# Two heads at a time in the attention of a two-block float32 transformer kernel

## The chip, the cores and the metric

One core of one Trainium2 chip. The metric is device microseconds of one execution of the whole kernel. The engines are named as in the profile: PE (TensorE matmul), PEld (TensorE weight load), DVE (VectorE), ACT (ScalarE), POOL (GpSimd), SP (SyncE, which issues the loads).

## What is computed

Two transformer blocks of two layers each, on 256 tokens of 1024 features. The second block has two streams (latent and context). Only the attentions matter here; each has 8 heads.

```python
# first block, kind 0: sliding window with sinks; kind 1: causal over one block of 256 tokens (both with ALiBi)
logits = einsum('bnqhgd,bnkhd->bnhgqk', q, k) * 64 ** -0.5      # 64 features a head
p = exp(logits - m); out = einsum('bnhgqk,bnkhd->bnqhgd', p / denom, v)
# second block, per stream: 96 features in q and k, 64 in v; the latent stream sees the context's keys too
s = einsum('bqhd,bkhd->bhqk', q, k) * 96 ** -0.5
o = einsum('bhqk,bkhd->bqhd', softmax(s), v)
```

In the second block attention runs three times: context (256 keys) and latent (512 keys) in layer 0, latent (512 keys) in layer 1. In layer 1 the context gives keys and values alone.

## The kernel before

All weights stream from memory in chunks of eight 128 x 128 tiles. `Weights.get` loads chunks ahead (SP), ACT rounds each to `wh` (L302) and DVE forms the rest `wl` (L261), three chunks ahead of use. A product of the stream (`mm3`) is three float32r matmuls of a weight tile with 256 or 512 tokens, so a chunk is 24 matmuls; all matmuls go through one helper and stand at L373.

Work that does not use weights runs on the side. `tick()` is called at each new chunk and moves every generator in `self.sides` one `yield` further; what a generator issues is put behind the last matmul of the stream (`issue_after`), and the framework's scheduler then sets the order of the instructions on each engine. `attn1` (L924) and `attn2` (L1285) are such generators. `finish` drives one to its end.

Before, `attn1` takes one head per tick. In tick s it issues the logits of head s (tile `lg`: a matmul with 128 and one with 256 columns, with 64 rows of the array, rows 0 to 63 or 64 to 127 by the head's partition `p0`), its softmax on DVE and ACT (`softmax_step`), the three 128 x 128 transposes of head s-2 (`pt`, L940) with ACT's copy to `pts`, and the values of head s-3 (`pv`: a matmul with 256 and one with 128 columns, whose 64 output columns of the array are 0 to 63 or 64 to 127 by `op`). Two heads share a bank of `pv`, which is split into `yah`, `yal` or `ych`, `ycl` after the second.

`attn2` takes one head and one block of 128 queries per tick, 16 in all: one or two logit matmuls of 256 columns on 96 rows, softmax, two or four transposes (L1313), two or four value matmuls of 128 columns into 64 output columns. These matmuls are float32: the profile shows each of them as two MATMUL records, and each transpose as one.

PSUM banks: `at` (logits) has 2 buffers, `st` (transposes) and `pv` one each, `mm` (the stream) four.

The lines of one tick of `attn1` that the text speaks of:

```python
self.mm(lg[:, :P], qa[:, :P], ka[:, :P], True, True)
self.mm(lg[:, P:], qa[:, P:], ka, True, True)
...
self.mm(o, v[0][:, vc:vc + 64], t[:, :T], True, False)
self.mm(o[:, P:], v[1][:, vc:vc + 64], t[:, 2 * P:], False, True)
```

Of the kernel before, what the change touches and what calls it, by code (L numbers as in the profile page):

```python
# [19 lines left out]
P = 128  # L20
D = 1024
# [13 lines left out]
# hidden tiles of the second block's first feed-forward that the context makes ahead, and its groups  # L35
# [4 lines left out]
# column tiles of the first block's w_in  # L40
# [3 lines left out]
# column tiles of the second block's w_in (kr padded to a tile)  # L44
# [4 lines left out]
# the order of the second block's branches (0: convolution, 1: attention, 2: Fourier)  # L49
# [3 lines left out]
# ---------------------------------------------------------------- layout on the host  # L53
# [5 lines left out]
def _chunks(blocks):  # L59
    """[n, 128, 128] tiles in order of use -> [n / 8, 128, 1024]"""  # L60
    a = np.concatenate(blocks, axis=0)
    n = a.shape[0]
    return a.reshape(n // 8, 8, P, P).transpose(0, 2, 1, 3).reshape(n // 8, P, 8 * P)


def _km(t, ms, ks=None):
    """k outer"""
    ks = range(t.shape[0]) if ks is None else ks
    return np.stack([t[k, m] for k in ks for m in ms])


def _mk(t, ms, ks=None):
    """k inner"""
    ks = range(t.shape[0]) if ks is None else ks
    return np.stack([t[k, m] for m in ms for k in ks])
# [26 lines left out]
def _head_cols(w, perm):  # L102
    """the columns of w in blocks of 64, permuted"""
    k, m = w.shape
    return w.reshape(k, m // 64, 64)[:, perm].reshape(k, m)
# [7 lines left out]
def _pack_weights(i):  # L113
    """all weights but w_ada, as tiles of 128 x 128 in the order in which the core uses them"""
# [48 lines left out]
def _cols(v):  # L163
    """a vector over features -> [128, n / 128]"""
    return v.reshape(-1, P).T
# [7 lines left out]
def _pack_vectors(i):  # L173
    """small vectors by partition; their columns by name"""
# [18 lines left out]
def _tables():  # L193
    """constants that depend on shapes alone"""
# [30 lines left out]
# ---------------------------------------------------------------- the program  # L225
class Weights:
    """The stream of weight chunks: loads and splits run ahead of the products."""
# [38 lines left out]
    def catch_up(self):  # L266
        """the split that was held back, if any"""
# [12 lines left out]
class Kernel:  # L280
# [12 lines left out]
    # -- instructions  # L293
# [42 lines left out]
    # -- order of work  # L336
    def after_root(self):
        """work that can wait stays out of the steps of a root"""
        return self.tc.issue_after(self.last_root.ins) if self.last_root else contextlib.nullcontext()
# [40 lines left out]
    # -- operands in two parts  # L380
    def split_pair(self, name, src, scale=1.0):
        """hi, lo [128, 2, 256] of scale * src"""
# [12 lines left out]
    def split_affine(self, hi, lo, src, bias):  # L395
        """of src + bias, bias by partition"""
# [3 lines left out]
    # -- products  # L400
    def linear(self, nm, xs, ks, done, first_outer=0, name="mm"):
        """nm column tiles of weights against xs (a list of (hi, lo) [128, 256] by k); two column
        tiles to a bank; done(i, bank, n) for each bank. The first first_outer tiles k outer."""
# [21 lines left out]
    def linear_tiles(self, xs, ks, done, name="mm", outer=False, hold=False):  # L425
        """as linear, for D features; done(m, psum) takes each column tile, the last two of which
        have a bank each; with outer, the first four go k outer; with hold, the
        split ahead of the last chunk is left to the norm that follows"""
# [21 lines left out]
    # -- statistics over features  # L450
    def rsqrt(self, nv, n=2, keep=False):
        """(-nv) ** -0.5 from the exponent's half by a step of third order, z' = z (u^2 + 10/3 s^2 u + 5 s^4)
        with u = nv z^2, and one of second order, z' = z (u + 3 s^2); each step's z is s times the root,
        with s' = 8/3 s^5 and s' = 2 s^3, 1 in the end"""
# [21 lines left out]
    def colsum(self, parts, tag="st"):  # L476
        """sums over partitions (features) of one or two tiles [128, 256]: [128 tokens, 2]"""
# [9 lines left out]
    def spread(self, out, v):  # L487
        """[128 tokens, 2] -> the same row of 256 tokens on all partitions"""
# [3 lines left out]
    # ------------------------------------------------------------ setup  # L492
    def setup(self):
# [3 lines left out]
        # x first  # L497
# [36 lines left out]
    def ada_plan(self, l, lo, hi, every, wait=None):  # L534
        """jobs that make columns lo to hi of layer l's modulation vectors: outputs on partitions,
        summed over k; one each `every` ticks"""
# [35 lines left out]
    def ada_ready(self, l, i):  # L572
        """what the i-th (shift, scale) of layer l is used as"""
# [12 lines left out]
    def ada_gate(self, l, i):  # L586
        """the i-th gate of layer l"""
# [23 lines left out]
    # ------------------------------------------------------------ feed-forward products  # L611
    def ffn_act(self, name, bank, tmp, j):
        """silu(gate) * up of one hidden tile (gate and up in one bank) into half j of tmp"""
# [4 lines left out]
    def ffn_single(self, name, xs, outer, add, before_last=lambda: None):  # L618
        """one stream of 256 tokens; add(m, psum) takes each part of the result"""
# [34 lines left out]
    def ffn_both(self, name, us, add, ctx_done=lambda: None):  # L654
        """both streams (512 tokens); us by k: (hi, lo) [128, 2, 256]"""
# [12 lines left out]
        def gu_outer(hs):  # L668
            """the context's stream first, then the latent one on the same weights"""
# [72 lines left out]
    def ffn_early(self, n, tiles):  # L742
        """the context's hidden tiles that fill the latent stream's n-th norm"""
# [14 lines left out]
    def ffn_rest(self, name, us, uc, add, ctx_done):  # L758
        """both streams, with the context's first hidden tiles made ahead"""
# [61 lines left out]
    # ------------------------------------------------------------ first block  # L821
# [3 lines left out]
    def layer_norm_add(self, m, psum, scale_x):  # L825
        """tile m of scale_x + psum; its deviation from the mean of the first six tiles"""
# [38 lines left out]
    def layer_norm_end(self, gname, bname, l, xs, last):  # L865
        """the norm; operands in two parts (or the last layer's result in f32), and the residual"""
# [29 lines left out]
    def softmax_step(self, kind, h, logits, cols, l):  # L896
        """rows of one head for both query blocks: [128 q, 128 + 256 keys]"""
# [26 lines left out]
    def attn1(self, kind, l, heads, q, k, v, out):  # L924
        """heads: (head, q pair, q half, partition, k, v columns, output tile, its partition)"""
        ps, pts, pv = {}, {}, {}
        n = len(heads)
        for s in range(n + 3):
            if s < n:
                h, qt, p0, kt = heads[s][:4]  # L930
                lg = self.bank("at", "lg").rearrange("p a b -> p (a b)")[:, :384]
                qa, ka = q[qt][p0:p0 + 64, :], k[kt][p0:p0 + 64, :]
                self.mm(lg[:, :P], qa[:, :P], ka[:, :P], True, True)
                self.mm(lg[:, P:], qa[:, P:], ka, True, True)
                ps[s] = self.softmax_step(kind, h, lg, 384, l)
            if 0 <= s - 2 < n:
                z = ps.pop(s - 2)
                pt = self.bank("st", "pt").rearrange("p a b -> p (a b)")[:, :384]
                for c, (a, b) in enumerate(((0, 0), (P, 0), (2 * P, 0))):
                    self.nc.tensor.transpose(pt[:, c * P:(c + 1) * P], z[:, a:a + P], self.ident)  # L940
                t = self.slot("pts").rearrange("p a b -> p (a b)")[:, :384]
                self.act(t, pt, AF.Copy)
                pts[s - 2] = t
            if 0 <= s - 3 < n:
                i = s - 3
                vc, ot, op = heads[i][4:]
                t = pts.pop(i)
                if i % 2 == 0:
                    pv[0] = self.bank("pv", "pv")[:, 0, :]
                o = pv[0][op:op + 64, :]  # L950
                self.mm(o, v[0][:, vc:vc + 64], t[:, :T], True, False)
                self.mm(o[:, P:], v[1][:, vc:vc + 64], t[:, 2 * P:], False, True)
                if i % 2 == 1:
                    self.split_into(out[0][ot // 2][:, ot % 2, :], out[1][ot // 2][:, ot % 2, :], pv[0])
            yield

    def mixer1(self, l, xs, xa):
        """the first block's mixer and its norm; xs: operands by k, xa: residual"""
# [61 lines left out]
        # gated short convolution  # L1020
# [47 lines left out]
        # branches, merged  # L1068
# [84 lines left out]
    # ------------------------------------------------------------ second block  # L1153
# [3 lines left out]
    def rms_add(self, s, h, last=False):  # L1157
        """one tile [128, 256] more of the sum of squares"""
# [25 lines left out]
    def ada_apply(self, s, i, h, b, hi, lo, ks=range(KD)):  # L1184
        """operands of norm(h) * g * (1 + scale) + shift"""
# [8 lines left out]
    def rms_all(self, s):  # L1194
        """the squares of an input that is all there"""
# [22 lines left out]
    def low_norm(self, name, src, nk, g, nfeat, key):  # L1218
        """operands of a norm over the latent features of src (f32 tiles [128, 256])"""
# [24 lines left out]
    def kv_values(self, xs):  # L1244
        """values by token: [128 tokens, 512] for each of two blocks"""
# [16 lines left out]
    def key_rope(self, src, kt, lat):  # L1262
        """the shared rotary key (rows 64-95 of src, its permuted copy in 96-127) to all heads"""
# [7 lines left out]
    def rope_rows(self, out, src):  # L1271
        """rows 64-95 of out [128, n, 256]: src * cos + permuted src * sin"""
# [12 lines left out]
    def attn2(self, q, keys, vals, out, first):  # L1285
        """q, keys: by pair of heads [96, 2, 256]; vals: blocks of 128 tokens [128, 512]"""
        nk = len(keys)
        scale = 96.0 ** -0.5
        n = 16
        ps, pts, pv = {}, {}, {}  # L1290
        for s in range(n + 3):
            while s < n and len(q) < max(s // 4 + 1, first):
                yield
            if s < n:
                h, qb = divmod(s, 2)
                lg = self.bank("at", "lg2")
                qa = q[h // 2][0:96, h % 2, qb * P:(qb + 1) * P]
                for c in range(nk):
                    self.mm(lg[:, c, :], qa, keys[c][h // 2][0:96, h % 2, :], True, True)
# [476 lines left out]
```

## Time and profile before

| what | value |
|---|---|
| three runs, median (lowest to highest) | 2974.29 us (2972.76 to 2975.88) |
| profiled execution, span | 2972.9 us, 1.4 us under the median of the runs |
| PE, PEld, DVE, ACT, POOL busy | 99%, 92%, 69%, 45%, 4% |
| granted clock of TensorE, mean | 0.997 |
| attention in the first block, layer 0 and 1 | 33.1 to 126.4 us, 509.3 to 602.3 us (start of its first and last burst of matmuls) |
| attention in the second block | 1355.2 to 1434.2, 1574.9 to 1673.9, 2584.6 to 2683.2 us |

No time of the profiled execution itself is given beside its span; the median stands 1.4 us above it, which is taken as what lies around the span. The busy time of PE is a sum of modelled durations that overlap, so what an instruction costs PE is read from the distance between the starts of the instructions around it.

### The profile page before, as it was taken

What the parts mean: (1) busy time and instruction counts of PE and PEld (TensorE: products, weight loads), DVE (VectorE), ACT (ScalarE), POOL (GpSimd) and SP (SyncE); (2) the same over time, 40 slices, a digit from 0 to 9 for tenths busy, and PEclk for the clock granted to TensorE, in tenths of its full rate; (3) what the DMA queues carried; (4) which work ended last, traced back from release to release, by engine and by line L of the source; (5) the groups of instructions that cost most, each with busy time, mean ns of one, the idle gap of its engine ahead of it and who ended that gap; (6) DMA issues with size and microseconds to landing.
All of it is one profiled execution on the core that took longest, in us unless ns stands there. A gap on an engine that the chain in (4) does not pass through costs nothing. (4 is left out here: it accounts for less than half of the span.)

```text
span 2972.9 us, 51535 instructions
## 1 busy us (share of the span) xinstructions
PE 2935.0 (99%) x21000; PEld 2731.8 (92%) x21000; DVE 2065.2 (69%) x3506; ACT 1340.9 (45%) x2100; POOL 108.1 (4%) x121
## 2 busy tenths in 40 slices
PE   8999999999999999999999999999999999999999
PEld 7899999799999999999998998888888888989998
DVE  6779667647756787788888685555675557867655
ACT  6545444644544422246556552222322224665444
POOL 1001001000001000010010000000100001000000
PEclk9999999999999999999999999999999999999999
DMA  7565655354655665544453353443354543425453
GB/s 260 174 230 171 224 197 169 114 170 157 203 181 170 226 226 169 167 157 142 157 177 107 129 181 132 134 135 120 104 188 162 169 156 114 163 93 164 163 184 107
DMA packets 134589, 486.66 MB, mean 164 GB/s; under 512 B 14928, under 2 KB 15184, under 8 KB 134352
## 3 DMA queue, kind: packets, MB, share of 16 engines
q1 hardware_dynamic: 133776, 482.58, 49.0%
q8 instruction: 165, 2.70, 0.4%
q10 hardware_dynamic: 576, 0.79, 0.1%
q14 instruction: 72, 0.59, 0.1%
HBM read 482.26 MB, written 1.05 MB: 163 GB/s over the span
## 5 line engine op out<-in xcount | busy, mean ns | idle before, releaser
L302 ACT ACTIVATE wh<-raw 128x1024 fp32r<-128x1024 f32 x765 | 809.5, 1059 | 1260.4 <-issue 272.2
L261 DVE TENSOR_TENSOR wl<-raw,wh 128x1024 fp32r<-128x1024 f32 x765 | 939.3, 1230 | 500.6 <-ACT wh L302 492.4
L547 DVE SCALAR_TENSOR_TENSOR junk<-ada,cb 128x1024 bf16<-128x1024 f32 x256 | 313.6, 1225 | 3.6 <-DMA ada<-in_w_ada_dram 1.4
L373 PE MATMUL f<-xh,wh 128*128 128x256 f32 x704 | 199.0, 283 | 0.0
L373 PE MATMUL f<-xl,wh 128*128 128x256 f32 x704 | 198.9, 283 | 0.0
L373 PE MATMUL f<-xh,wl 128*128 128x256 f32 x704 | 197.4, 280 | 0.0
L373 PE MATMUL g<-xh,wh 128*128 128x256 f32 x608 | 173.9, 287 | 8.5 <-ACT wh L302 7.0
L373 PE MATMUL g<-xh,wl 128*128 128x256 f32 x608 | 173.8, 286 | 0.7 <-DVE wl L261 0.7
L373 PE MATMUL g<-xl,wh 128*128 128x256 f32 x608 | 173.1, 285 | 0.6 <-DVE xl L308 0.6
L373 PE MATMUL bg<-wh,wh 128*128 128x256 f32 x576 | 168.5, 292 | 0.0
L373 PE MATMUL bg<-wh,wl 128*128 128x256 f32 x576 | 162.7, 282 | 0.0
L373 PE MATMUL bg<-wl,wh 128*128 128x256 f32 x576 | 162.1, 281 | 0.0
L373 PE MATMUL b<-uh,wh 128*128 128x512 f32 (+1 forms) x384 | 145.7, 380 | 0.0
L373 PE MATMUL a<-uh,wh 128*128 128x512 f32 (+1 forms) x384 | 145.4, 379 | 0.0
L373 PE MATMUL a<-wh,wl 128*128 128x256 f32 x512 | 144.9, 283 | 0.0
L373 PE MATMUL a<-wh,wh 128*128 128x256 f32 x512 | 144.7, 283 | 0.0
L373 PE MATMUL a<-uh,wl 128*128 128x512 f32 (+1 forms) x384 | 144.1, 375 | 0.0
L373 PE MATMUL b<-uh,wl 128*128 128x512 f32 (+1 forms) x384 | 144.0, 376 | 0.0
L373 PE MATMUL a<-ul,wh 128*128 128x512 f32 (+1 forms) x384 | 143.7, 374 | 0.0
L373 PE MATMUL a<-wl,wh 128*128 128x256 f32 x512 | 143.5, 280 | 0.0
L373 PE MATMUL b<-ul,wh 128*128 128x512 f32 (+1 forms) x384 | 143.4, 374 | 0.0
L1169 POOL TENSOR_TENSOR sq<-sq,sq 128x256 f32<-128x256 f32 x63 | 64.5, 1030 | 2143.2 <-ACT sq L302 2141.9
(429 smaller groups left out, 8774.2 us busy)
## 6 DMA issues: line engine op xcount, KB each, us to landing
raw<-in_w_dram SPq DMA_DIRECT2D x765, 512.0 KB, 3.3
ada<-in_w_ada_dram SPq DMA_DIRECT2D x144, 512.0 KB, 3.9
hc<-in_ctx_dram SPq DMA_DIRECT2D x8, 256.0 KB, 6.0
x<-in_x_dram SPq DMA_DIRECT2D x4, 256.0 KB, 6.9
out_dram<-out SPq DMA_DIRECT2D x4, 256.0 KB, 2.4
cb<-in_c_dram SPq DMA_DIRECT2D x1, 512.0 KB, 8.3
cb<-in_c_ctx_dram SPq DMA_DIRECT2D x1, 512.0 KB, 8.4
dft<-in_dft_dram ACTq DMA_DIRECT2D x2, 256.0 KB, 4.2
```

The lines of the kernel that those rows point to most:

```text
L261: self.last_split = kb.nc.vector.tensor_tensor(lo.rearrange("p a b -> p (a b)"), raw, f.bitcast(F32), ALU.subtract)
L302: return self.nc.scalar.activation(out, in_, func, **kw)
L373: return self.nc.tensor.matmul(out, a, b, start=start, stop=stop)
L547: self.nc.vector.scalar_tensor_tensor(junk, raw, 1.0, self.cb[:, s, :], ALU.mult, ALU.mult, accum_out=self.mods[:, l, s, c:c + 1])
L1169: self.nc.gpsimd.tensor_tensor(r["q"], r["q"], q[:, 0, :], ALU.add)
```

## The change

`attn1` takes a pair of heads every two ticks. In the first tick of a pair it issues four logit matmuls that alternate between the two heads (one on rows 0 to 63, one on rows 64 to 127, each head into a bank of its own), both softmaxes, the transposes of the first head of the pair before, and the four value matmuls of the pair before that, which alternate between the two heads (output columns 0 to 63 and 64 to 127). The second tick has the transposes of the second head alone. `while self.ticks % 2 != kind` lets the two attentions of a layer begin their pairs on different ticks. `attn2` does the same with the two heads of `hp` on one block of queries: its logits are not alternated (96 rows), its values are, chunk by chunk. The same instructions are issued in all; elsewhere only line numbers, comments and docstrings differ. The core of the diff:

```diff
     def attn1(self, kind, l, heads, q, k, v, out):
-        ps, pts, pv = {}, {}, {}
-        n = len(heads)
-        for s in range(n + 3):
+        ps, pts = {}, {}
+        n = len(heads) // 2
+
+        def turn(i):
+            z = ps.pop(i)
+            pt = self.bank("st", "pt").rearrange("p a b -> p (a b)")[:, :384]
+            for c in range(3):
+                self.nc.tensor.transpose(pt[:, c * P:(c + 1) * P], z[:, c * P:(c + 1) * P], self.ident)
+            t = self.slot("pts").rearrange("p a b -> p (a b)")[:, :384]
+            self.act(t, pt, AF.Copy)
+            pts[i] = t
+
+        while self.ticks % 2 != kind:
+            yield
+        for s in range(n + 2):
             if s < n:
-                h, qt, p0, kt = heads[s][:4]
-                lg = self.bank("at", "lg").rearrange("p a b -> p (a b)")[:, :384]
-                qa, ka = q[qt][p0:p0 + 64, :], k[kt][p0:p0 + 64, :]
-                self.mm(lg[:, :P], qa[:, :P], ka[:, :P], True, True)
-                self.mm(lg[:, P:], qa[:, P:], ka, True, True)
-                ps[s] = self.softmax_step(kind, h, lg, 384, l)
+                pair = heads[2 * s:2 * s + 2]
+                lgs = [self.bank("at", "lg").rearrange("p a b -> p (a b)")[:, :384] for _ in pair]
+                for qa, ka in (((0, P), (0, P)), ((P, T), (0, T))):
+                    for (h, qt, p0, kt, *_), lg in zip(pair, lgs):
+                        o = lg[:, :P] if qa[0] == 0 else lg[:, P:]
+                        self.mm(o, q[qt][p0:p0 + 64, qa[0]:qa[1]], k[kt][p0:p0 + 64, ka[0]:ka[1]], True, True)
+                for j in range(2):
+                    ps[2 * s + j] = self.softmax_step(kind, pair[j][0], lgs[j], 384, l)
+            if 0 <= s - 1 < n:
+                turn(2 * s - 2)
             if 0 <= s - 2 < n:
...
-                self.mm(o, v[0][:, vc:vc + 64], t[:, :T], True, False)
-                self.mm(o[:, P:], v[1][:, vc:vc + 64], t[:, 2 * P:], False, True)
-                if i % 2 == 1:
-                    self.split_into(out[0][ot // 2][:, ot % 2, :], out[1][ot // 2][:, ot % 2, :], pv[0])
+                pair = heads[2 * s - 4:2 * s - 2]
+                ts = [pts.pop(2 * s - 4 + j) for j in range(2)]
+                o = self.bank("pv", "pv")[:, 0, :]
+                for (*_, vc, ot, op), t in zip(pair, ts):
+                    self.mm(o[op:op + 64, :], v[0][:, vc:vc + 64], t[:, :T], True, False)
+                for (*_, vc, ot, op), t in zip(pair, ts):
+                    self.mm(o[op:op + 64, P:], v[1][:, vc:vc + 64], t[:, 2 * P:], False, True)
+                self.split_into(out[0][ot // 2][:, ot % 2, :], out[1][ot // 2][:, ot % 2, :], o)
             yield
+            if 0 <= s - 1 < n:
+                turn(2 * s - 1)
+            yield
...
     def attn2(self, q, keys, vals, out, first):
...
+                lgs = [self.bank("at", "lg2") for _ in range(2)]
+                for j in range(2):
+                    qa = q[hp][0:96, j, qb * P:(qb + 1) * P]
+                    for c in range(nk):
+                        self.mm(lgs[j][:, c, :], qa, keys[c][hp][0:96, j, :], True, True)
...
+            if 0 <= s - 1 < n:
+                turn(2 * s - 2)
             if 0 <= s - 2 < n:
...
                 for c in range(2 * nk):
...
+                    for j in range(2):
+                        self.mm(pv[64 * j:64 * j + 64, qb * P:(qb + 1) * P],
+                                vals[c][:, 64 * (2 * hp + j):64 * (2 * hp + j) + 64],
+                                ts[j][:, c * P:(c + 1) * P], c == 0, c == 2 * nk - 1)
...
             yield
+            if 0 <= s - 1 < n:
+                turn(2 * s - 1)
+            yield
```

What this moves on PE, at three places. The rows are PE's program (line, output<-inputs, size of the output); a float32 matmul is one row here and two records in the profile.

First block, layer 0, sliding window, the tick in which logits and values stand together. Before: one head's logits, then one head's values, then the stream (`g`).

```order
L373 MATMUL lg_568<-qk_381,qk_383 128x128
L373 MATMUL lg_568<-qk_381,qk_383 128x256
L373 MATMUL pv_595<-pts_530,va_390 64x256
L373 MATMUL pv_595<-pts_530,va_390 64x128
L373 MATMUL g_47_504<-xh_101,wh_423 128x256
```

The changed kernel at the same place (`lg_628` and `lg_629` are the two heads' banks):

```order
L373 MATMUL lg_628<-qk_381,qk_385 128x128
L373 MATMUL lg_629<-qk_381,qk_385 128x128
L373 MATMUL lg_628<-qk_381,qk_385 128x256
L373 MATMUL lg_629<-qk_381,qk_385 128x256
L373 MATMUL pv_676<-pts_551,va_390 64x256
L373 MATMUL pv_676<-pts_593,va_390 64x256
L373 MATMUL pv_676<-pts_551,va_390 64x128
L373 MATMUL pv_676<-pts_593,va_390 64x128
L373 MATMUL g_67_627<-xh_101,wh_474 128x256
```

Four matmuls of each kind now stand in a row, alternating between the heads; the tick after has neither logits nor values.

Second block, layer 0, latent stream, a tick in the middle. Before: one head's two logits, four transposes, four values, then the stream (`bg`).

```order
L373 MATMUL lg_1571_19809<-kt_15341,q_1469_19155 128x256
L373 MATMUL lg_1571_19809<-kt_18246,q_1469_19155 128x256
L1313 MATMUL pt_1577_19822<-ident,p_1557_19695 128x128 x4
L373 MATMUL pv_1568_19766<-pts_1567_19764,v_1096_16043 64x128
L373 MATMUL pv_1568_19766<-pts_1567_19764,v_1098_16052 64x128
L373 MATMUL pv_1568_19766<-pts_1567_19764,v_1427_18905 64x128
L373 MATMUL pv_1568_19766<-pts_1567_19764,v_1429_18914 64x128
L373 MATMUL bg_19804<-wh_17925,wh_19650 128x256
```

The changed kernel, from the second head's logits on:

```order
L373 MATMUL lg_1497_19319<-kt_15339,q_1444_19020 128x256
L373 MATMUL lg_1497_19319<-kt_18244,q_1444_19020 128x256
L1309 MATMUL pt_1508_19344<-ident,p_1481_19189 128x128 x4
L373 MATMUL pv_1510_19351<-pts_1488_19208,v_1096_16043 64x128
L373 MATMUL pv_1510_19351<-pts_1491_19262,v_1096_16043 64x128
L373 MATMUL pv_1510_19351<-pts_1488_19208,v_1098_16052 64x128
L373 MATMUL pv_1510_19351<-pts_1491_19262,v_1098_16052 64x128
L373 MATMUL pv_1510_19351<-pts_1488_19208,v_1427_18905 64x128
L373 MATMUL pv_1510_19351<-pts_1491_19262,v_1427_18905 64x128
L373 MATMUL pv_1510_19351<-pts_1488_19208,v_1429_18914 64x128
L373 MATMUL pv_1510_19351<-pts_1491_19262,v_1429_18914 64x128
L373 MATMUL bg_19297<-wh_17925,wh_19124 128x256
```

Eight value matmuls stand in a row and change the head at each; in 23 of the 24 pairs of the second block they stand so (with four where there are 256 keys), in one the first is apart.

First block, layer 0, sliding window, a later pair, while the values of the other attention are made (`cv`), in the changed kernel:

```order
L373 MATMUL pv_807<-pts_674,va_390 64x256
L935 MATMUL pt_713<-ident,z_529 128x128 x2
L373 MATMUL cv_751<-wh_597,xh_101 128x512
L373 MATMUL cv_751<-wl_598,xh_101 128x512
L373 MATMUL cv_751<-wh_597,xl_102 128x512
L373 MATMUL cv_752<-wh_597,xh_101 128x512
L373 MATMUL cv_752<-wl_598,xh_101 128x512
L373 MATMUL pv_807<-pts_717,va_390 64x256
L373 MATMUL pv_807<-pts_674,va_390 64x128
L373 MATMUL pv_807<-pts_717,va_390 64x128
```

Here the first head's matmul stands apart from the other three; so it is in 6 of the 16 pairs of the first block.

## Rows read from the trace of the kernel before

**Rows 1.** The page: its first line, and busy time of each engine.

```profile
span 2972.9 us, 51535 instructions
...
PE 2935.0 (99%) x21000; PEld 2731.8 (92%) x21000; DVE 2065.2 (69%) x3506; ACT 1340.9 (45%) x2100; POOL 108.1 (4%) x121
```

**Rows 2.** Waits of PE, whole span: waiter, releaser, us in total, times, longest.

```profile
PE pt L1313 <- ACT pts L302: 2.4, 2, 1.6
```

**Rows 3.** Timeline of PE, second block, last latent tick: start, us, line, operation.

```profile
1673.19 0.29 PE L373 MATMUL bg<-wl,wh 128*128 128x256 f32 x1
...
1673.67 0.28 PE L373 MATMUL bg<-wh,wl 128*128 128x256 f32 x1
1673.88 1.09 PE L373 MATMUL pv<-pts,v 128*64 128x128 f32 x8
...
1675.12 0.28 PE L373 MATMUL bg<-wl,wh 128*128 128x256 f32 x1
```

**Rows 4.** Timeline of PE, second block, last context tick.

```profile
1434.01 0.28 PE L373 MATMUL bg<-wh,wl 128*128 128x256 f32 x1
1434.21 0.65 PE L373 MATMUL pv<-pts,v 128*64 128x128 f32 x4
...
1435.02 0.28 PE L373 MATMUL bg<-wl,wh 128*128 128x256 f32 x1
```

**Rows 5.** Timeline of PE, second block, context, logits alone.

```profile
1359.88 0.29 PE L373 MATMUL f<-dft_h,fyl 128*128 128x256 f32 x1
1360.01 0.60 PE L373 MATMUL lg<-kt,q 96*128 96x256 f32 x2
...
1360.56 0.28 PE L373 MATMUL kn<-ckvl,wh 128*128 128x256 f32 x1
```

**Rows 6.** Timeline of PE, second block, latent, a tick in the middle.

```profile
1632.28 0.28 PE L373 MATMUL bg<-wh,wl 128*128 128x256 f32 x1
1632.39 1.03 PE L373 MATMUL lg<-kt,q 96*128 96x256 f32 x4
1633.26 0.60 PE L1313 MATMUL pt<-ident,p 128*128 128x128 f32 x4
1633.79 1.09 PE L373 MATMUL pv<-pts,v 128*64 128x128 f32 x8
...
1635.03 0.28 PE L373 MATMUL bg<-wl,wh 128*128 128x256 f32 x1
```

**Rows 7.** Timeline of PE, first block, logits alone.

```profile
36.77 0.28 PE L373 MATMUL g<-xh,wl 128*128 128x256 f32 x1
36.98 0.92 PE L373 MATMUL lg<-qk,qk 64*128 64x128 f32 x4
...
38.05 0.28 PE L373 MATMUL g<-xl,wh 128*128 128x256 f32 x1
```

**Rows 8.** Timeline of PE, first block, logits and values in one tick.

```profile
44.92 0.27 PE L373 MATMUL g<-xh,wl 128*128 128x256 f32 x1
45.13 0.92 PE L373 MATMUL lg<-qk,qk 64*128 64x128 f32 x4
45.98 0.86 PE L373 MATMUL pv<-pts,va 128*64 128x256 f32 x4
...
47.00 0.28 PE L373 MATMUL g<-xl,wh 128*128 128x256 f32 x1
```

**Rows 9.** Busy time by stretch, attention of the first block, layer 0.

```profile
core 0: us, PE busy (x) PEld busy (x) DVE busy (x) ACT busy (x) POOL busy (x), PEclk, DMA share, GB/s
33.00:60.00 27.00, 27.00 (x192) 23.16 (x191) 22.17 (x56) 19.30 (x49) 0.00 (x0) 1.00 0.61 209
```

**Rows 10.** Busy time by stretch, attention of the second block (same columns).

```profile
1575.00:1600.00 25.00, 22.53 (x170) 21.29 (x171) 24.38 (x49) 15.99 (x30) 0.00 (x0) 1.00 0.26 87
...
1627.00:1665.00 38.00, 38.00 (x285) 34.54 (x284) 20.06 (x42) 23.46 (x44) 0.00 (x0) 1.00 0.29 97
```

More of the change, by code (lines that the diff above doesn't have):

```diff
@@ L924, in attn1 @@
     def attn1(self, kind, l, heads, q, k, v, out):
-        ps, pts, pv = {}, {}, {}
-        n = len(heads)
-        for s in range(n + 3):
-            if s < n:
-                h, qt, p0, kt = heads[s][:4]
-                lg = self.bank("at", "lg").rearrange("p a b -> p (a b)")[:, :384]
-                qa, ka = q[qt][p0:p0 + 64, :], k[kt][p0:p0 + 64, :]
-                self.mm(lg[:, :P], qa[:, :P], ka[:, :P], True, True)
-                self.mm(lg[:, P:], qa[:, P:], ka, True, True)
-                ps[s] = self.softmax_step(kind, h, lg, 384, l)
-            if 0 <= s - 2 < n:
[L937 to L950, printed above, removed]
-                self.mm(o, v[0][:, vc:vc + 64], t[:, :T], True, False)
-                self.mm(o[:, P:], v[1][:, vc:vc + 64], t[:, 2 * P:], False, True)
-                if i % 2 == 1:
-                    self.split_into(out[0][ot // 2][:, ot % 2, :], out[1][ot // 2][:, ot % 2, :], pv[0])
@@ L1288, in attn2, with turn @@
         scale = 96.0 ** -0.5
[L1289 to L1292, printed above, removed]
+        n = 8
+        ps, pts = {}, {}
+        pv = None
+        def turn(i):
+            p = ps.pop(i)
+            pt = self.bank("st", "pt2").rearrange("p a b -> p (a b)")[:, :nk * T]
+            for c in range(2 * nk):
+                self.nc.tensor.transpose(pt[:, c * P:(c + 1) * P], p[:, c * P:(c + 1) * P], self.ident)
+            t = self.slot("pts2").rearrange("p a b -> p (a b)")[:, :nk * T]
+            self.act(t, pt, AF.Copy)
+            pts[i] = t
@@ L1293, in attn2 @@
+        for s in range(n + 2):
+            hp, qb = divmod(s, 2)
+            while s < n and len(q) < max(hp + 1, first):
                 yield
             if s < n:
[L1295 to L1299, printed above, removed]
-                lf = lg.rearrange("p a b -> p (a b)")[:, :nk * T]
@@ L1301, in attn2 @@
-                mx, nb, sm, rc = self.small("mx", 1), self.small("nb", 1), self.small("sm", 1), self.small("rc", 1)
-                self.nc.vector.tensor_reduce(mx, lf, AX.X, ALU.max)
-                self.ts(nb, mx, -scale, None, ALU.mult)
-                p = self.slot("p2").rearrange("p a b -> p (a b)")[:, :nk * T]
-                self.act(p, lf, AF.Exp, bias=nb, scale=scale, accum_out=sm)
-                self.nc.vector.reciprocal(rc, sm)
-                self.act(p, p, AF.Copy, scale=rc)
@@ L1308, in attn2 @@
-                ps[s] = p
+                lgs = [self.bank("at", "lg2") for _ in range(2)]
[4 more added lines that the diff above has]
+                for j in range(2):
+                    lf = lgs[j].rearrange("p a b -> p (a b)")[:, :nk * T]
+                    mx, nb, sm, rc = self.small("mx", 1), self.small("nb", 1), self.small("sm", 1), self.small("rc", 1)
+                    self.nc.vector.tensor_reduce(mx, lf, AX.X, ALU.max)
+                    self.ts(nb, mx, -scale, None, ALU.mult)
+                    p = self.slot("p2").rearrange("p a b -> p (a b)")[:, :nk * T]
+                    self.act(p, lf, AF.Exp, bias=nb, scale=scale, accum_out=sm)
+                    self.nc.vector.reciprocal(rc, sm)
+                    self.act(p, p, AF.Copy, scale=rc)
+                    ps[2 * s + j] = p
@@ L1309, in attn2 @@
+            if 0 <= s - 1 < n:
+                turn(2 * s - 2)
             if 0 <= s - 2 < n:
-                p = ps.pop(s - 2)
-                pt = self.bank("st", "pt2").rearrange("p a b -> p (a b)")[:, :nk * T]
+                hp, qb = divmod(s - 2, 2)
+                ts = [pts.pop(2 * s - 4 + j) for j in range(2)]
+                if qb == 0:
+                    pv = self.bank("pv", "pv2")[:, 0, :]
                 for c in range(2 * nk):
-                    self.nc.tensor.transpose(pt[:, c * P:(c + 1) * P], p[:, c * P:(c + 1) * P], self.ident)
@@ L1314, in attn2 @@
-                t = self.slot("pts2").rearrange("p a b -> p (a b)")[:, :nk * T]
-                self.act(t, pt, AF.Copy)
-                pts[s - 2] = t
-            if 0 <= s - 3 < n:
-                i = s - 3
-                h, qb = divmod(i, 2)
-                t = pts.pop(i)
-                if i % 4 == 0:
-                    pv[0] = self.bank("pv", "pv2")[:, 0, :]
-                r = 64 * (h % 2)
-                o = pv[0][r:r + 64, qb * P:(qb + 1) * P]
-                for c in range(2 * nk):
-                    self.mm(o, vals[c][:, 64 * h:64 * h + 64], t[:, c * P:(c + 1) * P], c == 0, c == 2 * nk - 1)
-                if i % 4 == 3:
-                    j = i // 4
-                    self.split_into(out[0][j // 2][:, j % 2, :], out[1][j // 2][:, j % 2, :], pv[0])
+                    for j in range(2):
+                        self.mm(pv[64 * j:64 * j + 64, qb * P:(qb + 1) * P],
+                                vals[c][:, 64 * (2 * hp + j):64 * (2 * hp + j) + 64],
+                                ts[j][:, c * P:(c + 1) * P], c == 0, c == 2 * nk - 1)
@@ L1330, in attn2 @@
+                if qb == 1:
+                    self.split_into(out[0][hp // 2][:, hp % 2, :], out[1][hp // 2][:, hp % 2, :], pv)
+            yield
+            if 0 <= s - 1 < n:
+                turn(2 * s - 1)
             yield
```

## Prediction

> **What bounds the kernel now.** I read the page first: PE is busy 2935.0 of the 2972.9 us of the span, every other engine less [rows 1]. Then PE's waits: the longest entry that concerns attention is two waits of 2.4 us in all [rows 2]. So attention costs what its matmuls take in PE's stream. The busy times are modelled and overlap, so next I read the timeline of PE around attention and took distances between starts. What the reader is to see there:
>
> The stream goes on at 0.12 us a matmul (1673.19 to 1673.67 is four of them [rows 3]). For a burst of attention I take the start of the last matmul of the stream before it and that of the second one after it, less two times 0.12. Eight records of values then cost 1.45 - 0.24 = 1.21 us [rows 3], four cost 1.01 - 0.24 = 0.77 [rows 4]. The difference of four is 0.44: a record of 128 columns takes **0.11 us**, and 0.33 us is left over in both. That is the price of a **visit**: going from the full array to 64 output columns and back. Two records of 256 columns on 96 rows cost 0.68 - 0.24 = 0.44 [rows 5], 0.22 each with nothing left over, so a visit is not the price of float32, nor of leaving the stream. A whole tick agrees: 2.75 - 0.24 = 2.51 us [rows 6] against 4 x 0.22 + 4 x 0.11 + 8 x 0.11 + 0.33 = 2.53. In the first block logits alone cost 1.28 - 0.24 = 1.04 us [rows 7]; their four records are 2 x 0.11 + 2 x 0.22 = 0.66, so a visit to 64 rows costs 0.38. Logits and values back to back cost 2.08 - 0.24 = 1.84 [rows 8], 0.52 over 2 x 0.66: one joint visit.
>
> **The change, part by part.** It removes and adds no instruction on PE, ACT, DVE or SP; it puts two heads together. Three things follow.
>
> *Fewer visits.* The pieces are counted in PE's program. First block, before: 32 groups of logits and 32 of values, of which 12 ticks have logits, transposes, values (0.38 + 0.33 = 0.71 each), six have both back to back (0.52), 14 have logits alone (0.38), 14 values alone (0.33): 8.5 + 3.1 + 5.3 + 4.6 = 21.6 us. After: 16 groups of logits and 22 of values (six pairs are torn in two, because the second head's transposes come late): five of 0.71, three of 0.52, eight of 0.38, 14 of 0.33 = 12.8 us. Gain 8.8. Second block: 48 groups of values become 25; 23 x 0.33 = 7.6. Together **16.4 us**.
>
> *Two heads on two halves of the array.* Neighbouring matmuls now use different halves: rows for the logits of the first block, output columns for all values. Before has no two neighbours like that, so no row shows what the second one costs. Bounds: its full time (nothing gained), or nothing (it lies wholly beside its neighbour). PE starts matmuls in the order of its program (no other order shows in [rows 3 to 8]), and each float32 matmul is two records on the same half, so I let a record begin as soon as its half is free and the record before it has begun. Four logits of a pair are records A A B B A A B B with 0.11, 0.11, 0.11, 0.11, 0.22, 0.22, 0.22, 0.22: the second A beside the first B, and so on, 0.88 us in place of 1.32, 0.44 less. Values of the first block the same, 0.44 less, and 0.22 less where the pair is torn. In the second block 8 records take five places of 0.11 and 16 take nine: 0.33 and 0.77 less. Sum: logits 16 x 0.44 = 7.0; values of the first block 10 x 0.44 + 6 x 0.22 = 5.7; of the second 8 x 0.33 + 16 x 0.77 = 15.0, less 0.1 for the torn pair: **27.6 us**. I take this value, not the upper bound, because the order of the program allows no more; the lower bound is rival A.
>
> *Longer bursts, other work late.* Two softmaxes enter DVE and ACT in one tick, none in the next. What is queued behind them there is the split of weights (`wh`, `wl`), made three chunks ahead; PE waits for it only if that lead is used up. In the middle of the second block's attention DVE is busy 20.06 of 38 us and ACT 23.46 [rows 10], in the first block 22.17 and 19.30 of 27 [rows 9]; if PE's part shrinks by 2 of 27 us there is still room. One stretch has none: at 1575 to 1600 us DVE is busy 24.38 of 25 and PE only 22.53 [rows 10]; but there logits of 96 rows and the stream stand, of which the change takes nothing off PE's path. The transposes follow their logits by two ticks, as before; only the second head's come a tick later, and its copy to `pts` still has a tick before the values. Cost taken: 0; rival C is what it costs if that cover is gone. The loads on SP's queue and the jobs on POOL keep their ticks: 0. Starting kind 0 and 1 on ticks of different parity delays an attention by one tick at most; both are done many ticks before the branches read them: 0.
>
> **Sum.** 16.4 + 27.6 = 44.0 us. The profiled span of 2972.9 becomes 2928.9; the runs' median stands 1.4 higher, so 2974.3 - 44.0 = **2930 us**.
>
> **The rivals.**
>
> A. *The halves don't run side by side*; then the change doesn't do what it says, and only the visits are saved: 2974.3 - 16.4 = 2958. For it: nothing in the trace shows two matmuls at once. Against it: PE visibly changes its form for 64 rows and 64 columns (0.38 and 0.33 us), so it does treat the halves as parts.
>
> B. *Pairs run wholly together*: logits 16 x 0.66, values 10 x 0.66 + 6 x 0.22, and 8 x 0.44 + 16 x 0.88, 36.1 us in place of 27.6: 2974.3 - 52.5 = 2922. Against it: the two records of one head follow each other.
>
> C. *Softmax becomes the late wait.* Both heads' rows go through DVE and ACT one behind the other, so transposes or values stand waiting at the front of PE's queue. The price of one is in the trace: 1.2 us on average [rows 2]. If ten of the 40 pairs pay it, 12 us go back: 2942. Against it: only two such waits in 80 heads' ticks of before.
>
> [...]
>
> E. *Row halves run together, column halves don't*: 16.4 + 7.0 = 23.4 less, 2951. For it: the two column halves share all 128 rows, so the loads of one head's weights cross rows in which the other's matmul runs. Against it: in the stream a weight load of all rows precedes every matmul, PEld is busy 92% [rows 1], and still the pace is 0.12 us [rows 3]; loads lie under matmuls of the same rows.
>
> [...]
>
> **How the numbers follow.** Chances: the forecast 0.48, A 0.18, B 0.08, C 0.12, D 0.08, E 0.06. The range reaches from B, less 2 us, to A plus 4 for waits: 2920 to 2962, all but D and the worse ends of A and C. A measurement of this kernel tells 0.2%, 6 us, from no change. Faster by more than that are the forecast, B, E, nearly all of C and A unless waits take 10 us of its 16: 0.85. Within it: D with a small price (0.04 to 0.09 us), A or C at their worst: 0.07. Slower: D above that, or waits at every pair: 0.08.
>
> **What would show it.** [...] Logits of a pair with their visit: 0.88 + 0.38 = 1.26 (1.70 under A). Of the gain, some 11 us should lie in each layer of the first block and 5, 9 and 9 us in the three attentions of the second. Waits of PE for `pts` or `wl` that sum to over 8 us would make C true. A saving outside attention, or distances as in A with a time near 2930, would make the argument wrong even with the right number.

## The result and the profile after

The changed kernel takes **2923.08 us** (median of 4 runs, 2921.71 to 2924.28), the kernel before, run beside it, 2975.09 (2972.76 to 2975.99): a ratio of 0.9825, with a 95% interval of 0.9811 to 0.9839. The gain is 52.0 us where 44.0 were forecast. The direction is right and the time lies in the range, but the number is that of rival B, whose sum was 52.5.

The page's head and its busy times, after; they answer to [rows 1].

```profile
span 2919.9 us, 51534 instructions
...
PE 2882.8 (99%) x21000; PEld 2699.4 (92%) x21000; DVE 2060.6 (71%) x3506; ACT 1336.2 (46%) x2100; POOL 109.0 (4%) x121
```

The span is 53.0 us shorter, and PE, with as many matmuls as before, is busy 52.2 us less and still bounds the kernel. The others do the same work in a shorter time, so their shares rise a little.

PE's waits on attention after, to be set against [rows 2] (columns: waiting engine, tile and line, releaser, us in total, times, longest):

```profile
PE pt L1309 <- ACT pts L302: 0.8, 1, 0.8
PE pt L935 <- ACT z L302: 0.7, 2, 0.5
```

They sum to 1.5 us. PE doesn't wait longer than before, so the gain must be read from the distances in its stream, in the way of the prediction: from the start of the last matmul of the stream to that of the second one behind the burst, less 0.24. Timeline of PE after, the last visit of the latent attention and that of the context, against [rows 3] and [rows 4]:

```profile
1630.36 0.27 PE L373 MATMUL bg<-wh,wl 128*128 128x256 f32 x1
1630.56 1.09 PE L373 MATMUL pv<-pts,v 128*64 128x128 f32 x16
...
1631.80 0.28 PE L373 MATMUL bg<-wl,wh 128*128 128x256 f32 x1
...
1401.09 0.28 PE L373 MATMUL bg<-wh,wl 128*128 128x256 f32 x1
1401.30 0.66 PE L373 MATMUL pv<-pts,v 128*64 128x128 f32 x8
...
1402.11 0.28 PE L373 MATMUL bg<-wl,wh 128*128 128x256 f32 x1
```

The 16 records of two heads cost 1631.80 - 1630.36 - 0.24 = **1.20 us**. Before, the eight records of one head cost 1.21 [rows 3]: the second head costs nothing. Eight records cost 0.78, as four did (0.77 [rows 4]). A latent tick, two groups of logits and one visit, against [rows 6]:

```profile
1603.37 0.28 PE L373 MATMUL bg<-wh,wl 128*128 128x256 f32 x1
1603.48 1.89 PE L373 MATMUL lg<-kt,q 96*128 96x256 f32 x8
1605.21 0.60 PE L1309 MATMUL pt<-ident,p 128*128 128x128 f32 x4
1605.74 1.09 PE L373 MATMUL pv<-pts,v 128*64 128x128 f32 x16
...
1606.99 0.28 PE L373 MATMUL bg<-wl,wh 128*128 128x256 f32 x1
```

3.62 - 0.24 = 3.38 us. By the prices of before it is 8 x 0.22 + 4 x 0.11 + 8 x 0.11 + 0.33 = 3.41: the logits on 96 rows still cost each record in full, the values only one head's. First block, logits alone and logits with values, against [rows 7] and [rows 8]:

```profile
77.97 0.28 PE L373 MATMUL b<-xh,wl 128*128 128x256 f32 x1
78.18 0.93 PE L373 MATMUL lg<-qk,qk 64*128 64x128 f32 x8
...
79.26 0.28 PE L373 MATMUL b<-xl,wh 128*128 128x256 f32 x1
...
46.95 0.28 PE L373 MATMUL g<-xh,wl 128*128 128x256 f32 x1
47.17 0.93 PE L373 MATMUL lg<-qk,qk 64*128 64x128 f32 x8
48.02 0.87 PE L373 MATMUL pv<-pts,va 128*64 128x256 f32 x8
...
49.05 0.28 PE L373 MATMUL g<-xl,wh 128*128 128x256 f32 x1
```

Logits of a pair 1.05 us, logits and values of a pair 1.86, where one head took 1.04 and 1.84: here too a pair costs what one head did. A narrow window counts the records that run in it; two of them from the start of the latent visit (1605.7 to 1605.8 and to 1605.95) show how the halves keep step:

```profile
1605.74 0.33 PE L373 MATMUL pv<-pts,v 128*64 128x128 f32 x2
...
1605.74 0.44 PE L373 MATMUL pv<-pts,v 128*64 128x128 f32 x4
```

Both heads' records begin together, from the first on (1605.744 and 1605.751, 1605.905 and 1605.911), and not, as the prediction had it, one place apart.

Summed over all bursts of attention, with the same measure (forecasts rounded, so that they add up to 45):

| stage | before, us | after, us | gain | forecast |
|---|---|---|---|---|
| first block, layer 0 | 39.4 | 28.4 | 11.0 | 11 |
| first block, layer 1 | 37.7 | 23.1 | 14.6 | 11 |
| second block, context | 22.8 | 17.0 | 5.9 | 5 |
| latent | 42.2 | 31.9 | 10.4 | 9 |
| last latent | 41.9 | 33.3 | 8.6 | 9 |
| sum | 184.1 | 133.7 | 50.4 | 44 |

So 50.4 of the span's 53.0 us come from attention. (In the first block some bursts stand beside matmuls of 512 columns, which start 0.23 us apart and not 0.12; this puts the sums of both kernels up by one to two us, their difference by less than 0.5.) The other 2.6 us I could not place.

### The profile page after: what moved, and what is told of

It reads as the page before. It is cut to its first block, busy times and chain, and to the rows that moved or that the text cites. A ratio compares the mean times of both kernels' runs of the same rounds, so it can differ in the third digit from the quotient of the medians.

```text
span 2919.9 us, 51534 instructions
## 1 busy us (share of the span) xinstructions
PE 2882.8 (99%) x21000; PEld 2699.4 (92%) x21000; DVE 2060.6 (71%) x3506; ACT 1336.2 (46%) x2100; POOL 109.0 (4%) x121
## 3 DMA queue, kind: packets, MB, share of 16 engines
HBM read 482.26 MB, written 1.05 MB: 166 GB/s over the span
```

## The experiments

The theory (T1 where an expectation numbers the theories): records on two halves run wholly beside each other, in whatever order they stand. Its rivals: they do so only because the two heads stand in turn (T2); or the halves add little to the saved visits (A of the prediction), or only the row halves share (E). Each kernel is an edit of the changed one. Both heads on one half, only the logits on one half, head after head and two pairs in a visit ran on one chip, with 2972.96 us for the kernel before (7 runs, 2971.39 to 2975.64). The other four, the changed kernel again among them, ran on another chip, with 2973.52 us (9 runs).

**Both heads on one half.** The logits of both heads use rows 0 to 63 (in the first block) and the values of both use output columns 0 to 63, the values head after head, so only the saved visits are left. The values' bank then holds the second head beside the first, and its split is four instructions in place of two.

```diff
-                        self.mm(o, q[qt][p0:p0 + 64, qa[0]:qa[1]], k[kt][p0:p0 + 64, ka[0]:ka[1]], True, True)
+                        self.mm(o, q[qt][0:64, qa[0]:qa[1]], k[kt][0:64, ka[0]:ka[1]], True, True)
...
+                    self.mm(o[0:64, op // 64, :], v[0][:, vc:vc + 64], t[:, :T], True, False)
+                    self.mm(o[0:64, op // 64, P:], v[1][:, vc:vc + 64], t[:, 2 * P:], False, True)
+                self.split_halves(out[0][ot // 2][:, ot % 2, :], out[1][ot // 2][:, ot % 2, :], o)
...
+                        self.mm(pv[0:64, j, qb * P:(qb + 1) * P],
```

> As the kernel with logits on one half, and the values of both heads go to output columns 0 to 63 too, into two halves of a bank, head after head; the split then takes two instructions on ACT and on DVE in place of one, and the second head's low part is formed from the wrong high part. So pairs and visits are as in the changed kernel, and nothing runs side by side. Theory: values cost 10 x 0.66 + 6 x 0.22 + 8 x 0.44 + 16 x 0.88 = 25.5 us more beside the 10.6 of the logits: 2959 us, so the saved visits are worth 16 us of the 52. Rival (fewer visits are worth nothing, the overlap is all): 2975 us. Rival (the overlap is worth little, visits or a better order of the other engines are the gain): under 2940 us.

Measured: 2957.57 us (2955.48 to 2959.63), ratio 0.9947 (0.9930 to 0.9964). Timeline of PE, last latent visit:

```profile
1658.15 0.28 PE L373 MATMUL bg<-wh,wl 128*128 128x256 f32 x1
1658.36 1.96 PE L373 MATMUL pv<-pts,v 128*64 128x128 f32 x16
...
1660.47 0.28 PE L373 MATMUL bg<-wl,wh 128*128 128x256 f32 x1
```

The same 16 records cost 2.32 - 0.24 = 2.08 us on one half, 16 x 0.11 + 0.33, against 1.20 on two. The time is near the theory's 2959 and far from both rivals. The visits alone are worth 2972.96 - 2957.57 = 15.4 us (10.7 to 20.8 by the interval); the term said 16.4.

**Only the logits on one half.** The values keep their two column halves.

```diff
-                        self.mm(o, q[qt][p0:p0 + 64, qa[0]:qa[1]], k[kt][p0:p0 + 64, ka[0]:ka[1]], True, True)
+                        self.mm(o, q[qt][0:64, qa[0]:qa[1]], k[kt][0:64, ka[0]:ka[1]], True, True)
```

> The changed kernel, but in the first block both heads' logits are made on rows 0 to 63, from the first head's q and k (so the second head's logits are not its own). Theory (two halves run wholly side by side): the eight records of a pair's logits take 1.32 in place of 0.66 us beside their visit, 16 x 0.66 = 10.6 us more: 2934 us. Rival (what was gained in the logits is the saved visits alone): nothing changes, 2923 us.

Measured: 2933.26 us (2932.13 to 2934.20), ratio 0.9866 (0.9852 to 0.9881). Timeline of PE, first block, logits alone:

```profile
80.34 0.28 PE L373 MATMUL b<-xh,wl 128*128 128x256 f32 x1
80.55 1.57 PE L373 MATMUL lg<-qk,qk 64*128 64x128 f32 x8
...
82.28 0.28 PE L373 MATMUL b<-xl,wh 128*128 128x256 f32 x1
```

The time agrees with the theory's 2934 us. A pair's logits take 1.70 us against 1.05: 0.65 a pair, all of one head's 0.66, which over 16 pairs is 10.4. Between this kernel and the one above only the values' column halves differ (and their split): 2957.57 - 2933.26 = 24.3 us. That the column halves don't share (E) is out, and with it A. The changed kernel, in its other two sets of runs, is 9.0 and 10.2 us below this one, as the 10.4 say.

**Head after head.** The halves stay, but a head's matmuls stand in a row.

```diff
-                for qa, ka in (((0, P), (0, P)), ((P, T), (0, T))):
-                    for (h, qt, p0, kt, *_), lg in zip(pair, lgs):
+                for (h, qt, p0, kt, *_), lg in zip(pair, lgs):
+                    for qa, ka in (((0, P), (0, P)), ((P, T), (0, T))):
...
-                for (*_, vc, ot, op), t in zip(pair, ts):
...
-                for c in range(2 * nk):
-                    for j in range(2):
+                for j in range(2):
+                    for c in range(2 * nk):
```

> The changed kernel, but the matmuls of a pair are no longer alternated: first all logits (or values) of one head, then all of the other. Theory 1: each half of the array works off a list of its own, so the order of the program does not matter; a latent visit of 16 value records stays at 1.21 us and the kernel at 2924 us (1.3 us lost where torn pairs no longer share a visit). Theory 2: a matmul starts only when the matmul before it in the program has started, and a float32 matmul counts as one with both its records; then logits of a pair take 0.88 in place of 0.66 us, whole value pairs of the first block 1.10 in place of 0.66, 16 value records 1.54 in place of 0.88 us, eight 0.66 in place of 0.44: 21.6 us more, 2945 us.

Measured: 2932.19 us (2930.92 to 2933.37), ratio 0.9863 (0.9848 to 0.9878), between the two theories: neither holds as stated. Context visits, with four records of a head in a row, cost what they do alternating (the context's attention sums to 17.0 us in both), but a visit of 8 + 8 records doesn't. Timeline of PE, the last of those:

```profile
1633.67 0.28 PE L373 MATMUL bg<-wh,wl 128*128 128x256 f32 x1
1633.88 1.58 PE L373 MATMUL pv<-pts,v 128*64 128x128 f32 x16
...
1635.61 0.28 PE L373 MATMUL bg<-wl,wh 128*128 128x256 f32 x1
```

1.70 us: between 1.20 (together) and 2.08 (one after the other). Two windows of an earlier visit, from before its start to 1608.05 and to 1608.10, show where the second head comes in:

```profile
1607.59 0.65 PE L373 MATMUL pv<-pts,v 128*64 128x128 f32 x4
...
1607.59 0.82 PE L373 MATMUL pv<-pts,v 128*64 128x128 f32 x6
```

Up to 1608.05 only four records have begun, all of the first head; then the fifth and, 6 ns behind it, the first of the second head, which is the ninth in the program. So 4 + 8 = 12 places, 12 x 0.11 + 0.33 = 1.65, and 0.05 more, to which the next experiment comes back. The two latent attentions lose 35.7 - 31.9 and 37.0 - 33.3, together 7.5 of the 7.9 to 9.1 us that this kernel is behind the two results of the changed one. The 0.4 to 1.6 us left over are 0.1 us or less, an estimate, for each of the 16 pairs of logits of the first block, which also have four records of a head in a row. From this came a new theory, the rule of four: **a record may begin beside the one that stands four before it in the program, and no sooner**. By it up to four records of a head in a row cost nothing.

**Two and three matmuls of a head in turn** test that rule: four records in a row should cost nothing, six should cost two places. The edit, with 2 or 3 (here 3), is in the second block alone:

```diff
-                for c in range(2 * nk):
-                    for j in range(2):
+                for j, c in [(j, c) for a in range(0, 2 * nk, 3) for j in range(2) for c in range(a, min(a + 3, 2 * nk))]:
```

> The changed kernel, but in the second block two value matmuls (four records) of one head and then two of the other are issued. Theory (a half of the array takes up to four records ahead of the program's order, as the visit of 8 + 8 records showed, where the second head began with the fifth record of the first): nothing is lost, 16 records stay at 1.21 us, 2923 us. Rival (the second head begins late by what the first has in a row, less a fixed time that was met only by chance at four): some 0.2 us more a visit, 1.4 us, 2926 us.

> The changed kernel, but three value matmuls (six records) of one head, then three of the other, then one of each; with 256 keys there are only two of each. Theory (up to four records ahead): with 512 keys the second head begins with the third record of the first, 0.22 us late, and never makes that up: 16 records take 1.10 + 0.33 = 1.43 us, 16 x 0.22 = 3.5 us more, 2927 us; with 256 keys eight records stay at 0.77. Rival (any order is fine up to six records): 1.21 us and 2923.

Measured, one run each, so that the distances say more than the times: 2924.24 and 2929.13 us. Timelines of PE, the last latent visit by two and then by three:

```profile
1632.68 0.28 PE L373 MATMUL bg<-wh,wl 128*128 128x256 f32 x1
1632.88 1.14 PE L373 MATMUL pv<-pts,v 128*64 128x128 f32 x16
...
1634.18 0.28 PE L373 MATMUL bg<-wl,wh 128*128 128x256 f32 x1
```

```profile
1633.55 0.28 PE L373 MATMUL bg<-wh,wl 128*128 128x256 f32 x1
1633.76 1.36 PE L373 MATMUL pv<-pts,v 128*64 128x128 f32 x16
...
1635.28 0.28 PE L373 MATMUL bg<-wl,wh 128*128 128x256 f32 x1
```

By two a visit costs 1.26, by three 1.49 us; by three the second head's first record begins 6 ns behind the first head's third (1608.415 and 1608.409), four places later in the program, as the rule has it. The order of the sizes is the rule's, but both visits are some 0.05 us longer than its count of places (8 x 0.11 + 0.33 = 1.21 and 10 x 0.11 + 0.33 = 1.43), as is that of head after head.

The traces, read record by record, show where these 0.05 us come from. The first record of a half in a visit is followed by the second on that half after 0.16 us (above, 1605.744 and 1605.905); all later ones of the changed kernel's whole visits follow after 0.11. When both halves start together, this is paid once and lies in the 0.33. Head after head and by three the second half starts late and pays it again. By two both start together, but the second head's fifth record (1633.384) is followed by its sixth only after 0.153 us. Its weight load starts at 1633.375, 9 ns before it and 4 ns behind the start of the record that stands four before it in the program (1633.371); the load of a later record of a half otherwise starts some 0.1 us ahead of it. Head after head and by three, the first load of the half that starts late stands in the same way 4 ns behind the record four before it (1608.082 and 1608.078, 1608.413 and 1608.409).

The rule of four holds in the 15 whole visits of 16 records of each of the three kernels: no record begins before the one four before it, and some begin before the one three before it. By three the bursts of attention sum to 137.9 us, 133.8 in the control below: 4.1 of the 4.9 us by which the kernel is behind it.

**The control**: the changed kernel again, unedited.

> The changed kernel once more, beside the three others of this call: 2923 us, 0.9825 of before.

Measured: 2924.27 us (2923.50 to 2925.63), ratio 0.9835 (0.9821 to 0.9848), the first result again within 1.2 us.

**Two pairs in a visit.** If a visit is a fixed price, half as many are cheaper still. Values wait until two pairs have theirs ready; in the second block:

```diff
-                for c in range(2 * nk):
-                    for j in range(2):
...
                 if qb == 1:
+                    pv = self.bank("pv", "pv2")[:, 0, :]
+                    for qb in range(2):
+                        ts = [pts.pop(2 * (2 * hp + qb) + j) for j in range(2)]
+                        for c in range(2 * nk):
+                            for j in range(2):
```

> The changed kernel, but the values of two pairs are made in one visit: in the first block of two pairs of heads (two visits an attention), in the second of both blocks of queries of a pair (four visits an attention). Theory (a visit costs 0.33 us whatever is done in it): 12 visits less in the second block and some ten in the first, 7 us less: 2916 us. Rival (results of the transposes that are kept longer, and values that come in a lump, make other work late): same or up to 7 us more, 2923 to 2930 us.

Measured: 2918.34 us (2917.97 to 2919.23), ratio 0.9817 (0.9802 to 0.9831). Timeline of PE, last latent visit:

```profile
1626.51 0.28 PE L373 MATMUL bg<-wh,wl 128*128 128x256 f32 x1
1626.71 1.97 PE L373 MATMUL pv<-pts,v 128*64 128x128 f32 x32
...
1628.84 0.28 PE L373 MATMUL bg<-wl,wh 128*128 128x256 f32 x1
```

32 records in 2.33 - 0.24 = 2.09 us: 16 places and one 0.33. The price of a visit is the theory's, but the gain is 4.7 to 5.9 us against the two results of the changed kernel, where 7 were expected. In the second block the bursts sum to 2.4 us less, where 12 visits make 4.0. Transposes now meet waits for `pts` there, five of 1.5 us together, where the changed kernel has one of 0.8: the rival's late work came in part.

**Four steps in a visit** in the second block, and in the first block the transposes behind the values:

```diff
+                if (s - 2) % 4 == 3:
+                    pv = self.bank("pv", "pv2")
+                    for hp, qb in [(hp - 1, 0), (hp - 1, 1), (hp, 0), (hp, 1)]:
...
+                    self.split_into(out[0][hp // 2], out[1][hp // 2], pv)
```

> As the kernel with two pairs in a visit, but in the second block the values of four steps (two pairs of heads, both blocks of queries) are made in one visit, two visits an attention, and in the first block the transposes stand behind the values, so that logits and values share a visit. Theory (a visit has a fixed price, results can wait in the buffers): six visits less in the second block, 2.0 us, and some 1 us in the first: 5 to 8 us under the changed kernel of the same call, near 2916 us. Rival (up to eight transposed tiles wait at a time in 45 shared buffers, and 64 records of values come in a lump): the stream waits for buffers or weights and the kernel is at or above the changed one, 2923 to 2930 us.

Measured: **2916.55 us** (2915.13 to 2918.50), ratio 0.9808 (0.9795 to 0.9822); the control of the same chip took 2924.27, and the two ranges of runs don't meet. Timeline of PE, last latent visit:

```profile
1621.77 0.28 PE L373 MATMUL bg<-wh,wl 128*128 128x256 f32 x1
1621.98 3.71 PE L373 MATMUL pv<-pts,v 128*64 128x128 f32 x64
...
1625.85 0.28 PE L373 MATMUL bg<-wl,wh 128*128 128x256 f32 x1
```

64 records in 4.08 - 0.24 = 3.84 us, 32 places and 0.32: the price of a visit is the same for 8, 16, 32 and 64 records. This version is the fastest of all that ran; PE's waits for `pts` sum to 1.5 us in it.

## Why the prediction was right in direction and low in size

*What bounds the kernel*: right. PE is busy 99% of the span after as before, and 50.4 of 53.0 us were gained in bursts of attention.

*Fewer visits, 16.4 us*: right, 15.4 measured with both heads on one half. The price itself, 0.33 us, came out within 0.01 in the visits above with the heads in turn, of 8, 16, 32 and 64 records.

*Two halves beside each other, 27.6 us*: the mechanism was right and the term too small. The time lies in the range only because the range was drawn down to rival B. The step that failed is "a record begins as soon as its half is free and the record before it has begun", and with it "the order of the program allows no more". It lets the halves run one place apart, and gives a pair's logits 0.88 us and 16 records nine places, 9 x 0.11 + 0.33 = 1.32 us with their visit. The trace has both heads' records begin within 7 ns of each other from the first, 0.66 us for the logits and eight places, 1.20 us with the visit. The runs put 24.3 us on the values (the forecast had 20.6, rival B has 25.5) and 9.0 to 10.4 on the logits (forecast 7.0, B 10.6): 33.3 to 34.7 in all, where the term said 27.6. With 15.4 for the visits that is 48.7 to 50.1 of the 52.0 us gained. What is missing, 1.9 to 3.3 us, is about the difference between the sets of runs: the kernel before took 2.1 us less in the set of these experiments (2972.96) than in that of the result (2975.09).

I chose that order because before shows no other. But before has only neighbours on the same half, so its rows could not show what one half does while the other is occupied: they were no evidence for the order, and the chance of 0.08 for B was too low. No run shows that bound: with the heads in turn their records begin within 7 ns of each other, and head after head the ninth record began 6 ns behind the fifth and before the sixth. The limit that these visits show is four places in the program, not one.

*Late work, 0 us*: right. Waits of PE for the rows of attention sum to 1.5 us, where rival C needed over 8; 0.7 of them, for `z` in layer 0, are new. DVE is as full in its worst stretch as it was, 24.48 of 25 us (24.38 [rows 10]); busy times of two stretches after (us, then PE, PEld, DVE, ACT, POOL):

```profile
33.00:60.00 27.00, 26.29 (x209) 22.60 (x207) 24.48 (x60) 19.60 (x49) 0.00 (x0) 1.00 0.67 216
1540.00:1565.00 25.00, 23.39 (x180) 22.39 (x179) 24.48 (x48) 15.80 (x30) 0.00 (x0) 1.00 0.29 89
```

In the first of them, layer 0, DVE has risen from 22.17 [rows 9] to 24.48 of 27 us, so the room is smaller than the prediction had it; more than "2 of 27" went off PE's path. Layer 0 also gained 3.6 us less than layer 1. Its bursts stand in more pieces (33 against 22), and five of its eight pairs of values are torn in two, against one of eight in layer 1. A torn pair in layer 0, after:

```profile
74.06 0.28 PE L373 MATMUL b<-xh,wl 128*128 128x256 f32 x1
74.26 0.65 PE L373 MATMUL pv<-pts,va 128*64 128x256 f32 x2
...
75.06 0.28 PE L373 MATMUL b<-xl,wh 128*128 128x256 f32 x1
...
76.34 0.28 PE L373 MATMUL b<-xh,wh 128*128 128x256 f32 x1
76.61 0.86 PE L373 MATMUL pv<-pts,va 128*64 128x256 f32 x6
...
77.62 0.28 PE L373 MATMUL b<-xh,wl 128*128 128x256 f32 x1
```

It costs 0.76 + 1.04 = 1.80 us; a whole pair that stands alone, at 117.73 us, costs 0.99. By these two, four more torn pairs make some 3.2 of the 3.6 us, an estimate. The prediction counted six torn pairs rightly, but put the same 11 us on both layers. No run has layer 0 without its torn pairs.

*The rivals.* A and E fell with 2.08 us on one half against 1.20 on two: the two column halves, which share all 128 rows, ran beside each other. D of the chances, a price for every change of halves, fell with the visits of 16 records, which change halves with every matmul and cost 1.20 us, where one head's eight cost 1.21. B is what happened. C did not come.

## What to carry to other kernels

Price a matmul that uses part of the array in two parts, both from distances between starts in the stream: its records, and the change of form around them (here 0.33 us), which was paid once for a burst, whether of 8 or of 64 records; so collect as much work of one form as buffers allow (7.7 us under the changed kernel here). Put independent work on the other half and write it in turn, one matmul each: the second head's matmuls were then free (1.20 us for 16 records of two heads, 1.21 for eight of one), two each in turn cost 0.05 us a visit, and eight records of a head in a row gave back 0.50 of 0.88 us. And where the trace has no example of a situation, don't take the order that it shows elsewhere for a bound: the two ends stay open, and the chance goes to both.

## What was not expected of the hardware

Between the two column halves of the array records began out of the program's order, up to four places ahead: with eight in a row the second head began with the first head's fifth record (1.70 us a visit), with six with its third (1.49), with four at once (1.26). Between the two row halves four in a row cost 0.1 us a pair or less, an estimate (0.4 to 1.6 us over 16 pairs, head after head); longer rows were not tried there, nor other sizes and types.

The first record of a column half in a visit was 0.16 and not 0.11 us ahead of the second (1605.744 and 1605.905). Halves that started together paid these 0.05 us at the same time, inside the visit's 0.33. The three visits pay them once more: with eight and six in a row the second half starts late, and with four in a row its fifth record has its weights loaded late. That the four places bound the weight loads, and the matmuls only through them, fits all three but was not tested.
